# Joining the high and low halves of Strassen products into one 512-column matmul, on PSUM banks that ScalarE fills first

## The chip, the cores and the metric

One Trainium2 chip, one core of it. The metric is the device time of one execution in microseconds (us); lower is better.

## What is computed

A trunk of two layers over one sequence of 512 frames of width 1024. Each layer, cut to what matters:

```
h = x + 1/2 * SwiGLU_1(RMSNorm(x))            # 1024 -> 2 x 2816 -> 1024
u = RMSNorm(h);  u @ w_in -> conv B, C, V | q_down | kv_down | k_rope | gate_conv | gate_mla
h = h + W_o( sigmoid(gate_conv) * conv_branch + sigmoid(gate_mla) * attention_branch )
h = h + 1/2 * SwiGLU_2(RMSNorm(h))
h = h + sigmoid(RMSNorm(h) @ W_pg) * (p[i] @ W_pp)
```

and a last RMSNorm behind both. Everything is float32.

## The kernel before

Activations lie transposed: features on the 128 partitions, the 512 frames along the free dimension, eight tiles `h[0..7]` of 128x512 for the residual. To get float32 accuracy from the faster matmul type, each operand is split into a high part, which is its rounding to that type, and a low part, the remainder. ScalarE makes the high part (the cast at line 70 for weights, line 209 for activations) and VectorE the low one (line 71, line 210). A product of two such operands takes three matmuls: high·high, high·low and low·high (`mm3`, lines 217 to 219).

Weights stream from DRAM in pieces of 128x1024 (`Stream`, buffers `st`, ten of them), are split into `wh` and `wl` (four buffers each), and are used once.

The up and gate projections of the four FFNs, and the gate projections of the mixer, are done by Strassen's method (the variant with seven products and 15 additions) in *quads*: four weight quarters of 128x1024 (`Quad`), each product being 512 rows of weights by 256 output features by 256 frames. Quarters are combined on VectorE (lines 146, 151, 154, 157). The activation side is combined once a stage (`Halved`, which fills `ys[1]` to `ys[7]`). `Sevens.product` issues the 24 matmuls of one product at line 455, each with 256 columns: 4 row tiles, 2 column tiles `w`, 3 parts. `Sevens.step(n, j)` does product `j` of quad `n`. Three PSUM banks serve a quad: `b` gathers products 1, 6, 7 and 4 one after the other, `c` gathers 5 and 3, and `a` has product 2. In between ScalarE copies the running sum out (line 474, after 1, 5 and 6), and VectorE adds it to another bank (line 479) to make an output quarter. Then `finish` (FFN) or `gate` (mixer) scales by the norm's reciprocal root, `r`, applies Silu or Sigmoid, and for the FFN splits the result into `acts`.

Down projections (`down`, 512 columns, bank `pd`) are laid between the products: four feature tiles at a time for one output tile `m`, 12 matmuls. In the mixer `conv_out` (also 12 matmuls) has that place. The order of products is written out by hand: in the FFN loop, for quad `n + 1` and what is left of `n`, it is (n+1,1), (n,7), (n+1,5), (n,4), (n+1,2), (n+1,6), (n+1,3), with 12-matmul pieces after the second, third, fourth and sixth. A scheduler at build time fixes the final order on each engine from what it reckons to be ready, so that matmuls of neighbouring pieces can be interleaved.

The second FFN of each layer (stage names `b0`, `b1`) begins with Strassen products of quads 0 and 1 at once; the first FFN (`a0`, `a1`) and the mixer (`m0`, `m1`) begin with ordinary projections. `e0`, `e1` are the last step of a layer.

All eight PSUM banks are one pool of single tiles (`mp`, `PS`). SBUF has a pool `G` of 60 tiles of 128x512.

Stages on TensorE: a0 from 6.2 us, m0 from 352.6, b0 from 737.8, e0 from 1080.7, a1 from 1135.6, m1 from 1480.0, b1 from 1865.3, e1 from 2208.2.

## Time and profile before

| | |
|---|---|
| median of 3 runs | 2277.62 us (2277.31 to 2277.88) |
| profiled execution, first to last instruction | 2275.7 us (the profile has no other time of it) |
| TensorE matmuls | 14206, busy 2266.7 us |
| VectorE | 2544 instructions, busy 1816.1 us |
| ScalarE | 1751 instructions, busy 1163.2 us |
| Strassen matmuls (line 455) | 8232 of 256 columns |
| DMA | 223.28 MB, mean 98 GB/s |

How to read the rows below. A row of the timeline has start, duration, engine, line, operation, output<-inputs, shape; a bracket at the end has how long the engine sat idle before and what ended it. Matmuls are pipelined: a duration reaches past the start of the next one, so the time that a matmul takes of TensorE is the distance from its start to the next start. A row of a stretch (`A:B`) has its length and then, for each engine (PE, PEld, DVE, ACT, POOL, or those of one line only), the busy time and the number of instructions, and at the end the granted clock, the DMA share and GB/s. A group row has the line, what it does, xcount, and after the bar the busy time, the mean duration in ns and the idle time before. PE is TensorE, PEld its weight loads, DVE VectorE, ACT ScalarE, SP the queue that issues most DMAs.

### The profile page before, as it was taken

What the parts mean: (1) busy time and instruction counts of PE and PEld (TensorE: products, weight loads), DVE (VectorE), ACT (ScalarE), POOL (GpSimd) and SP (SyncE); (2) the same over time, 40 slices, a digit from 0 to 9 for tenths busy, and PEclk for the clock granted to TensorE, in tenths of its full rate; (3) what the DMA queues carried; (4) which work ended last, traced back from release to release, by engine and by line L of the source; (5) the groups of instructions that cost most, each with busy time, mean ns of one, the idle gap of its engine ahead of it and who ended that gap; (6) DMA issues with size and microseconds to landing.
All of it is one profiled execution on the core that took longest, in us unless ns stands there. A gap on an engine that the chain in (4) does not pass through costs nothing.

```text
span 2275.7 us, 34817 instructions
## 1 busy us (share of the span) xinstructions
PE 2266.7 (100%) x14206; PEld 2058.0 (90%) x14206; DVE 1816.1 (80%) x2544; ACT 1163.2 (51%) x1751; POOL 38.1 (2%) x42
## 2 busy tenths in 40 slices
PE   9999999999999999999999999999999999999998
PEld 8999988899888999998899999888998889999987
DVE  8877778877877988877798887767878689878766
ACT  7444445456745644444664444454567465444444
POOL 0000000000200000000000000000001000000000
PEclk9999999999999999999999999999999999999999
DMA  5333343134121333333223333422331214333321
GB/s 195 112 112 95 105 130 102 55 113 130 47 66 56 103 112 111 94 120 122 91 80 97 112 93 118 119 87 74 103 121 47 75 38 138 103 103 93 121 93 38
DMA packets 63375, 223.28 MB, mean 98 GB/s; under 512 B 7280, under 2 KB 7280, under 8 KB 63216
## 3 DMA queue, kind: packets, MB, share of 16 engines
q1 hardware_dynamic: 62640, 220.28, 30.7%
q8 instruction: 111, 1.82, 0.3%
q10 hardware_dynamic: 576, 0.79, 0.1%
q14 instruction: 48, 0.39, 0.1%
HBM read 218.94 MB, written 2.10 MB: 97 GB/s over the span
## 4 chain that ended last, share of the span: by engine, by line
PE 98%; DVE 1%; ACT 0%; issue 0%; DVEq 0%; ACTq 0%
PE a0pd L217 2%; PE a1pd L217 2%; PE b0pd L217 2%; PE b1pd L217 2%; PE b1pd L218 2%; PE b0pd L218 2%; PE a1pd L218 2%; PE a0pd L218 2%; PE b0pd L219 2%; PE a1pd L219 2%; PE a0pd L219 2%; PE b1pd L219 2%; PE m0mop L217 1%; PE m1mop L218 1%; PE m0mop L218 1%; PE e0gp L219 1%
## 5 line engine op out<-in xcount | busy, mean ns | idle before, releaser
L70 ACT CAST wh<-st 128x1024 fp32r<-128x1024 f32 (+1 forms) x458 | 476.8, 1044 | 567.2 <-issue 62.7
L71 DVE TENSOR_TENSOR wl<-st,wh 128x1024 fp32r<-128x1024 f32 (+1 forms) x459 | 555.1, 1211 | 155.0 <-ACT wh L70 154.2
L70 ACT CAST wh<-s 128x1024 fp32r<-128x1024 f32 x98 | 103.0, 1051 | 132.6 <-DVE s L151 8.9
L71 DVE TENSOR_TENSOR wl<-s,wh 128x1024 fp32r<-128x1024 f32 x98 | 119.3, 1218 | 13.5 <-ACT wh L70 13.5
L154 DVE TENSOR_TENSOR st<-st,s 128x1024 f32<-128x1024 f32 x49 | 59.9, 1222 | 1.2
L151 DVE TENSOR_TENSOR s<-s,st 128x1024 f32<-128x1024 f32 x49 | 59.7, 1218 | 0.2
L157 DVE TENSOR_TENSOR st<-st,st 128x1024 f32<-128x1024 f32 x49 | 59.6, 1217 | 0.1
L146 DVE TENSOR_TENSOR s<-st,st 128x1024 f32<-128x1024 f32 x49 | 59.6, 1216 | 0.1
L563 DVE SCALAR_TENSOR_TENSOR h<-b1pd,h 128x512 f32<-128x512 f32 x40 | 27.5, 688 | 10.4 <-PE b1pd L219 10.4
L563 DVE SCALAR_TENSOR_TENSOR h<-b0pd,h 128x512 f32<-128x512 f32 x40 | 27.5, 687 | 9.1 <-PE b0pd L219 9.1
L563 DVE SCALAR_TENSOR_TENSOR h<-a1pd,h 128x512 f32<-128x512 f32 x40 | 27.5, 687 | 7.6 <-PE a1pd L219 7.5
L563 DVE SCALAR_TENSOR_TENSOR h<-a0pd,h 128x512 f32<-128x512 f32 x40 | 27.4, 685 | 6.4 <-PE a0pd L219 6.4
L107 POOL MEMSET wh<- 128x256 f32 x4 | 1.1, 312 | 1189.7 <-DVE wl L71 1189.7
L988 ACT ACTIVATE e1g<-e1pg,e1r 128x512 f32<-128x512 f32 (+1 forms) x9 | 5.4, 641 | 11.9 <-PE e1pg L950 11.9
L992 DVE TENSOR_TENSOR e1g<-e1g,e1in 128x512 f32<-128x512 f32 (+1 forms) x9 | 5.7, 628 | 7.3 <-ACT e1g L988 7.3
L117 DVE TENSOR_TENSOR kl<-st,kh 128x512 fp32r<-128x512 f32 x8 | 5.3, 688 | 7.4 <-ACT kh L116 7.4
L882 DVE TENSOR_TENSOR m1g<-m1mop,m1g 128x512 f32<-128x512 f32 x8 | 5.5, 689 | 5.9 <-PE m1mop L219 5.9
L882 DVE TENSOR_TENSOR m0g<-m0mop,m0g 128x512 f32<-128x512 f32 x8 | 5.5, 689 | 5.5 <-PE m0mop L219 5.5
L300 ACT ACT_TABLE_LOAD x7 | 9.0, 1283 | 0.1
L287 DVE TENSOR_TENSOR e1acc<-e1acc,e1sq 128x512 f32<-128x512 f32 x7 | 4.8, 691 | 4.8 <-ACT e1sq L286 4.3
L709 DVE TENSOR_TENSOR m1g<-m1cop,m1g 128x512 f32<-128x512 f32 x8 | 5.5, 687 | 2.0 <-PE m1cop L219 2.0
L709 DVE TENSOR_TENSOR m0g<-m0cop,m0g 128x512 f32<-128x512 f32 x8 | 5.5, 687 | 2.0 <-PE m0cop L219 2.0
(11249 smaller groups left out, 8792.5 us busy)
## 6 DMA issues: line engine op xcount, KB each, us to landing
st<-in_weights SPq DMA_DIRECT2D x406, 512.0 KB, 3.5
h<-in_x SPq DMA_DIRECT2D x8, 256.0 KB, 5.3
st<-in_weights SPq DMA_DIRECT2D x7, 256.0 KB, 5.3
out<-e1d SPq DMA_DIRECT2D x4, 256.0 KB, 2.1
out<-fh SPq DMA_DIRECT2D x3, 256.0 KB, 2.2
e0pi<-in_p SPq DMA_DIRECT2D x2, 256.0 KB, 3.7
e1pi<-in_p SPq DMA_DIRECT2D x2, 256.0 KB, 3.7
fg<-in_final_row SPq DMA_DIRECT2D x2, 256.0 KB, 4.4
```

The source lines that it names most:

```text
L70: self.nc.scalar.copy(hi[:, w], src[:, w])
L71: last = self.nc.vector.tensor_tensor(lo[:, w], src[:, w], hi[:, w].bitcast(F32), ALU.subtract)
L146: tt(self.s, self.a21, self.a22, ALU.add)
L151: tt(self.s, self.s, self.a11, ALU.subtract)
L154: tt(self.a12, self.a12, self.s, ALU.subtract)
L157: tt(self.a11, self.a11, self.a21, ALU.subtract)
L217: nc.tensor.matmul(ps, wh, vh, start=first, stop=False)
L218: nc.tensor.matmul(ps, wh, vl, start=False, stop=False)
L219: nc.tensor.matmul(ps, wl, vh, start=False, stop=last)
L563: nc.vector.scalar_tensor_tensor(h[m], ps, 0.5, h[m], ALU.mult, ALU.add)
L709: nc.vector.tensor_tensor(gates[m], ps, gates[m], ALU.mult)
L882: nc.vector.tensor_tensor(t, mla_ps[m], t, ALU.mult)
```

## The change

In five of the seven products (1, 2, 3, 4, 6) the high weights meet high and low activations in one matmul of 512 columns, whose output fills a bank: 256 columns of sums with the high part, 256 with the low part. The low weights meet the high part in a second matmul of 256 columns, added onto the first half. Each bank of a product becomes a pair of banks (two column tiles), and an output quarter is the sum of the two halves (`out`: ScalarE copies one half, VectorE adds the other). Products 5 and 7 keep three matmuls of 256 columns (`product`).

Instead of adding a saved sum on VectorE, ScalarE copies the pair `b` onto the seeded pair (`seed`) after product 1 and again after product 6, and products 2, and 5 and 3, accumulate onto that copy. The combination of weight quarters for product 6 is formed in another way, so that 5 needs no `s`. The order in a quad becomes (n+1,1), (n,4), (n+1,2), (n+1,6), (n+1,5), (n+1,7), (n+1,3), with 12-matmul pieces after 1, 2, 6 and 3. The first two quads of the second FFNs (`early`) keep products 5 and 3 on a bank of their own and do product 3 as before.

PSUM is divided outside attention into two pairs for `b`, one seeded pair, and two single banks; inside attention it is eight single banks. High and low parts of the layer inputs, of the query latents, of the rotary key and of the head outputs lie side by side in eight paired buffers (`X`), and `G` has 44 tiles. The transposed probabilities of attention move from `G` to three raw weight buffers. The two halves of each `u` row are split separately. The end of an FFN, the head of the other stages and the order around the mixer's first quad are rearranged for the smaller number of single banks.

```diff
-N_BIG = 60
+N_BIG = 44
+N_PAIR = 8
...
 class Quad:
-    def __init__(self, W, quarters):
-        self.W = W
+    def __init__(self, W, quarters, early):
+        self.W, self.early = W, early
         for q in ("a11", "a21", "a22", "a12"):
             setattr(self, q, W.raw(quarters[q]))
         tt = W.nc.vector.tensor_tensor
         if j == 1:
             return W.split(self.a11)
         if j == 2:
             return W.split(self.a12)
-        if j == 6:
-            tt(self.s, self.s, self.a11, ALU.subtract)
-            return W.split(self.s)
+        if j == 4:
+            return W.split(self.a22)
         if j == 3:
             tt(self.a12, self.a12, self.s, ALU.subtract)
             return W.split(self.a12)
-        if j == 7:
+        if self.early:
+            if j == 5:
+                self.s = W.buffer("s")
+                tt(self.s, self.a21, self.a22, ALU.add)
+                return W.split(self.s)
+            if j == 6:
+                tt(self.s, self.s, self.a11, ALU.subtract)
+                return W.split(self.s)
             tt(self.a11, self.a11, self.a21, ALU.subtract)
             return W.split(self.a11)
-        return W.split(self.a22)
+        if j == 6:
+            tt(self.a11, self.a11, self.a21, ALU.subtract)
+            self.s = W.buffer("s")
+            tt(self.s, self.a22, self.a11, ALU.subtract)
+            return W.split(self.s)
+        if j == 5:
+            tt(self.a21, self.a21, self.a22, ALU.add)
+            return W.split(self.a21)
+        return W.split(self.a11)
...
+        def eight(self):
+            self.close()
+            self.single = self.pool("mp", 8)
+        def paired(self):
+            self.close()
+            self.chain, self.seeded, self.single = self.pool("bp", 2), self.pool("ap", 1), self.pool("mp", 2)
...
+    def two(pool, name):
+        return pool.tile([P, 1024], F32, tag="bb", name=name).rearrange("p (w t) -> p w t", t=512)
+    def PB(name):
+        return two(banks.chain, name)
+    def PA(name):
+        return two(banks.seeded, name)
+    def halves(t):
+        return [t[:, 0, :], t[:, 1, :]]
+    def X(name):
+        t = xp.tile([P, 1024], F32R, tag="x", name=name).rearrange("p (a t) -> p a t", t=S)
+        v = HiLo((t[:, 0, :], t[:, 1, :]))
+        v.pair = t
+        return v
...
+    def split(src, name, scale=None, paired=False):
+        v = X(name) if paired else (G(name + "h", F32R), G(name + "l", F32R))
+        split_to(*v, src, scale)
+        return v
...
+            self.ys[7].append((th[:, right], tl[:, right]))
+            for p_, at in ((2, left), (3, right)):
+                self.ys[p_].append(self.both(xs[k], at))
+            for p_, at in ((6, left), (4, right)):
+                v = G(f"{self.name}u{j}_{p_}", F32R).rearrange("p (a t) -> p a t", t=H)
+                last = split_to(v[:, 0, :], v[:, 1, :], u[:, at])
+                self.ys[p_].append((v[:, 0, :], v))
...
+        def joint(self, ps, d, j):
             hi, lo = d.pop(("part", j), None) or d["w"].part(j)
-            for k, (vh, vl) in enumerate(self.ys[j]):
+            for k, (vh, pair) in enumerate(self.ys[j]):
+                for w in range(2):
+                    at = slice((2 * k + w) * P, (2 * k + w + 1) * P)
+                    nc.tensor.matmul(ps[:, w, :].rearrange("p (a t) -> p a t", t=self.H), hi[:, at], pair, start=j == 1 and k == 0,
+                                     stop=False, skip_group_check=True)
+                    nc.tensor.matmul(ps[:, w, :self.H], lo[:, at], vh, start=False, stop=k == 3, skip_group_check=True)
+        def product(self, ps, d, j, start=False):
+            hi, lo = d.pop(("part", j), None) or d["w"].part(j)
+            for k, v in enumerate(self.ys[j]):
+                vh, vl = v if j in (5, 7) else (v[0], v[1][:, 1, :])
                 for w in range(2):
                     at = slice((2 * k + w) * P, (2 * k + w + 1) * P)
                     for i, (a_, b_) in enumerate(((hi, vh), (hi, vl), (lo, vh))):
-                        nc.tensor.matmul(ps[:, w, :], a_[:, at], b_, start=j in (1, 5, 2) and w + k + i == 0,
-                                         stop=w + k + i == 6, skip_group_check=True)
+                        nc.tensor.matmul(ps[:, w, :], a_[:, at], b_, start=start and w + k + i == 0,
+                                         stop=k == 3 and i == 2, skip_group_check=True)
+        def seed(self, n, what):
+            d = self.todo[n]
+            d[what] = PA(f"{self.name}{n}{what}")
+            nc.scalar.copy(d[what].rearrange("p w t -> p (w t)"), d["b"].rearrange("p w t -> p (w t)"))
+        def out(self, n, ps, f, c):
+            t = self.tile(n, f"o{f}{c}")
+            nc.scalar.copy(t, ps[:, :, self.H:])
+            nc.vector.tensor_tensor(t, ps[:, :, :self.H], t, ALU.add)
+            self.done(n, f, c, t, t)
         def step(self, n, j):
+            d, H, early = self.quad(n), self.H, n < self.early
+            tt = nc.vector.tensor_tensor
+            if j == 1:
+                d["b"] = PB(f"{self.name}{n}b")
+                self.joint(d["b"], d, j)
+                if not (early and n):
+                    self.seed(n, "a")
+            elif j == 2:
+                self.joint(d["a"], d, j)
+                self.out(n, d.pop("a"), 0, 0)
+                if n + 1 < self.early:
+                    self.seed(n + 1, "a")
+            elif j == 6:
+                self.joint(d["b"], d, j)
+                if early:
+                    d["u"] = [self.tile(n, f"u{w}") for w in range(2)]
+                    for w in range(2):
+                        nc.scalar.copy(d["u"][w], d["b"][:, :, w * H:(w + 1) * H])
+                    tt(d["c5"], d["c5"], d["u"][1], ALU.add)
+                else:
+                    self.seed(n, "d")
+            elif j == 5:
+                d["c5"] = self.tile(n, "c5")
+                if early:
+                    d["c"] = PS(f"{self.name}{n}c").rearrange("p (w t) -> p w t", t=H)
+                    self.product(d["c"], d, j, True)
+                    nc.scalar.copy(d["c5"], d["c"])
+                else:
+                    self.product(d["d"][:, :, H:], d, j)
+                    nc.scalar.copy(d["c5"], d["d"][:, :, H:])
+            elif j == 7:
+                self.product(d["b"][:, :, :H], d, j)
+                t = d.pop("c5")
+                tt(t, d["b"][:, :, :H], t, ALU.add)
+                self.done(n, 1, 1, t, t)
+            elif j == 3 and early:
+                self.product(d["c"], d, j)
+                t, l = d.pop("u")
+                tt(t, t, l, ALU.add)
+                tt(t, d.pop("c"), t, ALU.add)
+                self.done(n, 0, 1, t, t)
+            elif j == 3:
+                self.joint(d["d"], d, j)
+                self.out(n, d.pop("d"), 0, 1)
             else:
+                self.joint(d["b"], d, j)
+                self.out(n, d.pop("b"), 1, 0)
...
+        f_last = (np_ - 3) // 2 * 4
+        downs = []
+        def fill():
+            if downs:
+                m, f0 = downs.pop(0)
+                down(m, f0, f0 + 4)
+        def next_quad(n):
+            for i, j in enumerate((1, None, 4, 2, None, 6, None, 5, 7, 3, None)):
+                if j is None:
+                    if i < 10 or downs and downs[0][1] < f_last:
+                        fill()
+                    continue
+                step(n if j == 4 else n + 1, j)
+                if j == 6 and n % 2:
+                    downs.extend((m, 2 * n - 2) for m in range(KD))
...
+            behind = sums
+            for n, j in ((0, 2), (0, 6), (0, 3), (0, 7), (1, 2), (0, 4), (1, 6), (1, 3), (1, 7)):
+                with tc.issue_after(behind):
+                    step(n, j)
+                behind = W.last_split
+            n0 = 1
...
+        for n in range(n0, np_ - 1):
+            next_quad(n)
+        f0 = f_last
+        left = [m for m in range(KD) if (m, f0) in downs]
+        assert len(left) == len(downs)
+        spare = halves(PA(f"{name}pd"))
+        for m in left[:3]:
+            pds[m] = down(m, f0, f0 + 4, spare[0] if len(pds) == 2 else None, last=False)
+            if len(pds) == 1:
+                step(np_ - 1, 4)
+        if beside:
+            beside()
+        for m in left[3:4] + [m for m in range(KD) if m not in left[3:4]]:
+            if m in left[3:]:
+                down(m, f0, nf, spare[1] if m == left[3] else None)
+            else:
+                down(m, f0 + 4, nf, pds.get(m), first_=m not in pds)
...
+            pss = halves(PB(f"{name}{nm}p")) + [PS(f"{name}{nm}p2")]
+            return [proj(W.col("w_in", l, c0 + k * P, D), xs, None, pss[k]) for k in range(width // P)]
...
+            if last:
+                ys.row(k, xs)
+                step(0, 1)
...
+            if last:
+                step(0, 2)
+                step(0, 6)
...
+        for j in (5, 7, 3):
+            step(0, j)
...
+            for n_, j_, n_out in ((n + 1, 1, n > 0), (n, 4, 0), (n + 1, 2, 0), (n + 1, 6, 1), (n + 1, 5, 0), (n + 1, 7, 0),
+                                  (n + 1, 3, 1)):
                 step(n_, j_)
+                conv_outs(n_out)
+                if (n_, j_) == (n_last, 6):
+                    qc = [split(t, f"{name}qn{k}", paired=True) for k, t in enumerate(qt)]
                     kvc = [split(t, f"{name}kvn{k}") for k, t in enumerate(kvt)]
-                    krh, krl = split(krt, name + "kr")
-                if (n_, j_) == (n_last, 3):
-                    pairs[0].q_rope()
+                    krh, krl = split(krt, name + "kr", paired=True)
+        conv_outs(len(outs))
+        pairs[0].q_rope()
+        step(n_last, 4)
+        banks.eight()
...
+            return split(ps, n + "o", paired=True)
...
+        banks.paired()
         for m in range(KD):
             ps = proj(W.col("w_o", l, m * P, D), merged, f"{name}wop{m}")
...
+            pg, pp = halves((PA if m % 3 == 2 else PB)(f"{name}gp{m}"))
             proj(W.col("w_ple_gate", l, m * P, D), xs, None, pg)
```

More of the change, by code (lines that the diff above doesn't have):

```diff
@@ L321, in trunk_kernel @@
     nc.scalar.activation(warm, eps_t, AF.Copy)
-    idle = PS("idle")
-    for i in range(12):
-        nc.tensor.matmul(idle[:, :P], ones.bitcast(F32), ones.bitcast(F32), start=True, stop=True)
+    idle, one = PA("idle"), ones.bitcast(F32)
+    for i in range(8):
+        nc.tensor.matmul(idle[:, 0, :P], one, one, start=True, stop=True)
+    nc.tensor.matmul(idle[:, 1, :].rearrange("p (a t) -> p a t", t=P), one, one.unsqueeze(1).to_broadcast([P, 4, P]),
+                     start=True, stop=True)
     pt_w = [max(2, NT - j) * P for j in range(NT)]
@@ L384, in __init__, with both @@
             self.half = {}
+        @staticmethod
+        def both(v, at):
+            return v[0][:, at], v.pair[:, :, at]
         def row(self, j, xs):
@@ L400, in own @@
                 split_to(th[:, left], tl[:, left], t[:, left])
-            self.ys[1].append(tuple(v[:, left] for v in xs[j]))
+            self.ys[1].append(self.both(xs[j], left))
             self.ys[5].append((th[:, left], tl[:, left]))
@@ L443, in split @@
-        def split(self, n, j):
-            if n not in self.todo:
-                self.todo[n] = self.quad(n)
-            self.todo[n]["part", j] = self.todo[n]["w"].part(j)
-        def product(self, ps, d, j):
-            hi, lo = d.pop(("part", j), None) or d["w"].part(j)
-            for k, (vh, vl) in enumerate(self.ys[j]):
+            if n not in self.todo:
+                cs = self.columns(n)
+                quarters = {f"a{a_ + 1}{b_ + 1}": [(self.w, self.l, (4 * b_ + k) * P, c) for k in range(4) for c in cs[a_]]
+                            for a_ in range(2) for b_ in range(2)}
+                self.todo[n] = {"w": Quad(W, quarters, n < self.early)}
@@ L646, in lat_norm @@
             return ts
[L648 removed]
+        pkv = halves(PB(name + "kvp"))
+        projs([W.col("w_in", l, o_kv + k * P, D) for k in range(KL // P)], xs, pkv)
         pkr = PS(name + "krp")
@@ L884, in mixer @@
             merged.append(split(t, f"{name}mg{m}"))
+        banks.paired()
         for m in range(KD):
@@ L936, in ple_last @@
         name = f"e{l}"
+        banks.eight()
         pt = ple_parts(l, name)
```

250 lines of the change are left out of this document (106 added, 144 removed).

## The prediction

> **What bounds the kernel now.** I read the page's busy shares, clock row and chain first, then the waits of TensorE, then its timeline.
>
> ```profile
> span 2275.7 us, 34817 instructions
> ...
> PE 2266.7 (100%) x14206; PEld 2058.0 (90%) x14206; DVE 1816.1 (80%) x2544; ACT 1163.2 (51%) x1751; POOL 38.1 (2%) x42
> ...
> PEclk9999999999999999999999999999999999999999
> ...
> PE 98%; DVE 1%; ACT 0%; issue 0%; DVEq 0%; ACTq 0%
> ...
> PE idle L325 <- DVE hpi L255: 1.0, 1, 1.0
> ```
>
> TensorE is busy for the whole span at the full granted clock, 98% of the chain is its own work, and its one recorded wait is 1.0 us before the warm-up. So nothing another engine saves can show, and every nanosecond taken off a matmul does. A busy row is no proof that matmuls stand close together, since each lasts longer than its successor waits; the starts decide that:
>
> ```profile
> 300.48 0.40 PE L217 MATMUL a0pd<-a0a13h,wh 128*128 128x512 f32 x1
> ...
> 302.30 0.39 PE L219 MATMUL a0pd<-a0a15h,wl 128*128 128x512 f32 x1
> 302.53 0.28 PE L455 MATMUL a010a<-a0x4h,wh 128*128 128x256 f32 x1
> 302.64 0.28 PE L455 MATMUL a010a<-a0x4l,wh 128*128 128x256 f32 x1
> ...
> 1002.40 0.28 PE L455 MATMUL b09b<-b0u0h,wh 128*128 128x256 f32 x1
> ...
> 1005.28 0.40 PE L217 MATMUL b0pd<-b0a12h,wh 128*128 128x512 f32 x1
> 1005.51 0.40 PE L218 MATMUL b0pd<-b0a12l,wh 128*128 128x512 f32 x1
> ```
>
> From 1002.40 to 1005.28 lie the 24 matmuls of one Strassen product: 2.88 us, 120 ns each for 256 columns. From 300.48 to 302.30 lie 8 matmuls of 512 columns: 227.5 ns each. Twice the columns cost 107.5 ns more, so 12.5 ns of every matmul do not depend on its length. That is what the change attacks.
>
> **The change part by part.**
>
> *Fewer matmuls.* A product now has, for each of 4 row tiles and 2 column tiles, three 256-column matmuls (high·high, high·low, low·high). In a joint product the first two become one of 512 columns; the columns streamed stay the same.
>
> ```profile
> L154 DVE TENSOR_TENSOR st<-st,s 128x1024 f32<-128x1024 f32 x49 | 59.9, 1222 | 1.2
> ...
> 0.00:2276.00 2276.00, 1014.34 (x8232) 1009.95 (x8232) 1.00 0.31 98
> ```
>
> The first row (the subtraction of product 3, once a quad) counts 49 quads; the second is line 455 over the whole span, and its 8232 matmuls are 49 x 7 x 24. In 45 quads five products become joint. The first two quads of each second FFN keep product 3 as it was, so 4 quads have four. 45 x 5 + 4 x 4 = 241 joint products, 241 x 8 = 1928 matmuls gone. Inside runs of one length each is worth 12.5 ns, 24.1 us together. Joint products alternate lengths, so I look at the changes of length: behind a 512 the 256 takes 302.53 to 302.64, behind a 256 the 512 takes 1005.28 to 1005.51, so a pair is 0.34 us against 0.36, 20 ns saved, on starts rounded to 10 ns. I take 14 ns, nearer the value averaged over many instructions: 1928 x 14 = 27.0 us. Ends: 24.1 and, by the rounded starts, 38.6, which I do not believe.
>
> The Trainium skill, TensorE: Matmul & The Clock Gate, section "Wait — 56ns, not 53.3ns?", puts the fixed part of a warm matmul at about 2.5 ns. By that the 1928 would be worth an estimated 4.8 us. The trace disagrees: its starts leave 12.5 ns.
>
> *Seeds on ScalarE.* Each of the 45 quads gains two copies of two PSUM banks onto two others (after products 1 and 6), and swaps three 512-element copies for four. No row shows ScalarE writing PSUM. The nearest:
>
> ```profile
> 245.92 0.28 PE L455 MATMUL a08b<-a0u3h,wl 128*128 128x256 f32 x1
> 246.04 0.40 PE L217 MATMUL a0pd<-a0a8h,wh 128*128 128x512 f32 x1
> ...
> 248.79 0.28 PE L455 MATMUL a08c<-a0x4h,wh 128*128 128x256 f32 x1
> ...
> 246.17 1.05 ACT L70 CAST wh<-st 128x1024 fp32r<-128x1024 f32 x1 [0.94 <-PE a08b L455]
> ...
> 247.13 0.58 ACT L474 COPY a08c<-a08b 128x512 f32<-128x512 f32 x1
> ```
>
> A 1024-element cast takes 1.05 us and its successor starts 0.96 later; 512 from PSUM take 0.58; so I take 1.0 us for a seed, between 0.58 and twice that. These rows are also the pattern itself: a product on bank b ends at 245.92, a cast for later weights runs first, and the copy starts at 247.13. In the new order product 6 is followed by a down projection or a convolution output, 12 matmuls, here 246.04 to 248.79, and only then by product 5, which adds onto the seed. The seed would be ready at 248.13: 0.66 us to spare. The seed after product 1 has another product as cover as well. Cost 0, hidden by the 12 matmuls; above 1.66 us it would show. A gain is excluded, since the copy only adds a wait. ScalarE's extra is 45 x (2 x 1.0 + 0.58) = 116 us, and 4 for one seed in each of the four early quads, on 1163: 56%. Queued behind a late seed would be the next weight cast, which has three products of lead.
>
> *VectorE.* Each quad needs one more addition of 512 elements (four evacuations instead of three, product 4 included), and the same four subtractions on the weights.
>
> ```profile
> 0.00:2276.00 2276.00, 101.09 (x147) 1.00 0.31 98
> ...
> 800.00:1050.00 250.00, 250.00 (x1723) 233.65 (x1722) 199.74 (x242) 108.90 (x145) 0.00 (x0) 1.00 0.35 109
> ```
>
> The first row is line 479, 147 such additions: 0.69 us each, so 34 us more, 80% to 82%. The second is a steady FFN stretch (PE, PEld, DVE, ACT busy): VectorE at 199.74 of 250, with 8 quads in it some 5.5 more, still under 83%. Cost 0. Splitting each u row in two halves adds fixed parts on both engines for four rows a stage; taken at 0 inside the same slack.
>
> *Fewer single banks.* Eight PSUM banks in one pool become two pairs for bank b, one seeded pair and two singles outside attention. Where three singles are wanted within a few us, TensorE waits. Two places show it:
>
> ```profile
> 743.79 0.39 PE L297 MATMUL b0ps<-b0al,ones 128*128 128x512 f32 x1
> ...
> 746.90 0.28 PE L455 MATMUL b01c<-b0t0h,wh 128*128 128x256 f32 x1
> ...
> 748.27 0.70 ACT L302 ACTIVATE b0ms<-b0ps,eps_t 128x512 f32<-128x512 f32 x1
> ...
> 384.10 0.69 DVE L637 TENSOR_TENSOR m0qt<-m0qp,m0r 128x512 f32<-128x512 f32 x1 [0.67 <-PE m0qp L219]
> ...
> 384.36 0.40 PE L217 MATMUL m0Cp<-m0x0h,wh 128*128 128x512 f32 x1
> ...
> 386.56 0.68 ACT L302 ACTIVATE m0kvms<-m0kvps,eps_t 128x512 f32<-128x512 f32 x1
> ...
> 458.06 0.28 PE L455 MATMUL m0g0c<-m0t3h,wh 128*128 128x256 f32 x1
> 458.19 0.28 PE L455 MATMUL m0g1b<-m0x0h,wh 128*128 128x256 f32 x1
> ...
> 459.21 0.28 PE L455 MATMUL m0g1b<-m0x1h,wh 128*128 128x256 f32 x1
> 459.32 0.29 PE L455 MATMUL m0g0c<-m0t3l,wh 128*128 128x256 f32 x1
> ```
>
> At the head of the second FFN, bank c of quad 0 and the norm's sums hold both singles. The sums are last read at 748.27 + 0.70 = 748.97 behind a table load, while product 5 of quad 1 wants a bank at 746.90 - 0.1 (the joint product before it is shorter). That is 2.2 us, twice: 4.4. Ends 0 (TensorE's order is woven by readiness: from 458.19 to 459.21 seven matmuls of quad 1 stand between two of quad 0's bank c, so other products may fill the gap) and 4.4. In the mixer the first C projection (384.36) needs the third query bank, read until 384.79: 0.45 us, twice, 0.9; if it took the kv norm's bank, read until 386.56 + 0.68, 2.9 each. What then comes late is the weight cast behind it, with buffers to spare.
>
> *Attention.* It keeps eight banks. The head outputs now share eight paired buffers with the three query latents and the rotary key. Heads 0 to 3 find four free; 4 to 6 take those of the queries, done with once pair 3 is projected, ahead of head 4; head 7 takes the key's after the last scores.
>
> ```profile
> 548.00:658.00 110.00, 110.00 (x653) 98.43 (x651) 90.93 (x219) 77.50 (x174) 18.13 (x16) 1.00 0.20 63
> ...
> 564.95 0.28 PE L803 MATMUL m0s00p<-m0h0kn0h,m0h0qn0h 128*128 128x256 f32 x1
> ...
> 568.17 0.40 PE L217 MATMUL m0h1qr<-m0qn0h,wh 128*128 128x512 f32 x1
> ```
>
> The stage's VectorE is at 90.93 of 110, ScalarE at 77.50, TensorE without a gap. I take 0, hidden by that order; the upper end is one set of score matmuls (564.95 to 568.17, 3.2 us) waiting once for heads 4 and 7 of each layer, 12.9, should their late buffers hold up banks.
>
> *Order and DMA.* Products move to 1, 4 of the last quad, 2, 6, 5, 7, 3; the same transfers are issued on SP's queue, quarters are released earlier than before (a21 after product 5), and three of the ten raw buffers serve attention, where DMA is 0.20 busy. Cost 0, hidden by that slack. The warm-up has the same TensorE time.
>
> *The sum.* Against the profiled span: 2275.7 - 27.0 + 4.4 + 0.9 = 2254.0. The median of the runs, 2277.62, lies 1.9 above the span, so 2255.9; I say 2256.
>
> **The rivals.**
>
> *Partly eaten by banks.* The mechanism holds, but the attention end (12.9) and the kv bank (4.9 more) are paid, in all 17.8 or in good part: 2262 to 2273. For it: two singles instead of eight. Against: the same weaving.
>
> *Little of the fixed part goes.* If most of the 12.5 ns belongs to something that the 512 still pays (its two halves come from two runs), say all but a fifth, 24.1 / 5 = 4.8 us are saved, and 2277.6 - 4.8 + 5.3 = 2278, no change. Against: contiguous 512s pay it once, at 227.5 ns. The Trainium skill's 2.5 ns (TensorE: Matmul & The Clock Gate, the section above) would end here too.
>
> *Two pieces stream no faster than two matmuls.* The moving operand of a joint product 1, 2 or 3 is two runs of 256 columns, 512 apart; no row shows such a one. If the 512 then costs 240 ns, nothing is saved: 2277.6 + 5.3 = 2283. Against: the operand is contiguous within each run.
>
> *Slower: the seed after product 6 comes late.* Place: product 5 of 45 quads. It costs 45 us for each us that the seed exceeds 1.66; the 21.7 us left of the gain are gone at 1.66 + 0.48 = 2.14 us. If a copy into PSUM takes 2.4 us, or as much ScalarE work stands ahead of it, 45 x 0.74 = 33 us: 2289. For it: no price is known, and every quad repeats it. Against: 0.58 us for half as much.
>
> **How the numbers follow.** Main case 64% (2250 to 2262, its own range), partly eaten 14%, better than 2250 3%: faster 81%. Smaller fixed part 4%, stalls that cancel the gain 2%: within 0.2% (4.6 us, about what a measurement of this kernel can tell) 6%. Two pieces 4%, late seed 9%: slower 13%. The range 2249 to 2271 takes in the main case and nearly all of the eaten one.
>
> **What would show it.** Right: TensorE's count near 12,270 and joint pairs at 0.346 us; TensorE without waits before product 5; a gap near product 5 of quad 1 at the head of each second FFN. Wrong: gaps before products 2, 5 or 3 that repeat every quad, seed copies above 1.7 us, 512-column matmuls of joint products 240 ns apart, or gaps in the attention stage.

## The result, and the profile after

The changed kernel takes 2320.35 us (median of 4 runs, 2317.42 to 2320.87) against 2277.6: a ratio of 1.0185, 95% interval 1.0172 to 1.0197. It is 43 us slower; 2256 was forecast, and 2271 was the upper end. Its profiled execution spans 2318.8 us, 43.1 more than that of before.

Busy shares, clock and chain of the profile's page after:

```profile
span 2318.8 us, 31379 instructions
...
PE 2273.8 (98%) x12272; PEld 1960.4 (85%) x12272; DVE 1853.1 (80%) x2628; ACT 1270.3 (55%) x1922; POOL 40.4 (2%) x42
...
PE 90%; DVE 6%; ACT 2%; issue 1%; DMA 0%; SPq 0%; ACTq 0%; DVEq 0%
```

1934 matmuls are gone, and yet TensorE's busy time is 7 us higher: the matmuls that are left take longer, part of them at half clock, as shown below. The chain tells where else to look: VectorE now holds 6% of it, for 1%. The waits of TensorE after (waiting tile and line, what ended it: us in total, times, longest us):

```profile
PE a02b L530 <- DVE a0u L272: 7.4, 4, 2.7
PE m0kvp L281 <- DVE wl L72: 5.9, 1, 5.9
PE m0h0kn L279 <- DVE m0g3o L553: 3.5, 1, 3.5
PE b11c L542 <- ACT b1ms L363: 1.8, 1, 1.8
PE b01c L542 <- ACT b0ms L363: 1.8, 1, 1.8
PE e0gp L279 <- DVE e0g L1077: 1.4, 1, 1.4
```

Before there was one row of 1.0 us. None of these is at product 5 or 2 of a steady quad, where the forecast looked for the danger: they stand where stages begin. The third kind of loss is the clock (stretch, length, busy time and instructions of PE, PEld, DVE, ACT, POOL, granted clock, DMA share, GB/s):

```profile
52.00:62.00 10.00, 7.04 (x18) 5.16 (x19) 8.54 (x20) 6.29 (x12) 0.00 (x0) 0.50 0.01 2
369.00:377.00 8.00, 6.25 (x16) 4.95 (x17) 5.70 (x6) 1.33 (x3) 0.56 (x2) 0.57 0.60 199
```

Behind waits the granted clock drops to half: at 51.9 us for 10.2 us, at 369.4 for 6.8, at 577.6, 775.5 and 1912.2 for 3.4 each; before, none did between the warm-up and the last 6 us. The Trainium skill, TensorE: Matmul & The Clock Gate, section "What's actually happening", gives half rate after an idle window of about 3.4 us, with windows that run freely. The trace agrees with the windows: the starts and ends of these five stretches lie on one grid of 3.413 us. It adds that less idle time can do: at 775.5 and at 1912.2 a single wait of 1.8 us, with no other in the 9 us ahead, was enough; behind the same waits of e2, below, the clock stayed full.

To share out the 43.1 us I took the distance from every matmul's start to the next and compared it with the 227.5 ns (512 columns) and 120 ns (256) of undisturbed runs. The counts alone save 24.1 us. Against that stand 42.0 us more in gaps of over 40 ns, 13.8 us of half clock, and 12.3 us of small excess; the first matmul of a0 comes 1.0 earlier. (How much of a wait inside a half-clock stretch is called a gap is a choice: another count gives 45.9 and 9.9 in place of 42.0 and 13.8, with the same sum.) By stage the gaps grew by 7.0 us in a0, 12.7 in m0, 9.5 in b0, 9.3 in b1, and by nothing in a1, where the forecast's picture held: that stage went from 344.4 to 342.1 us.

### The profile page after: what moved, and what is told of

Same layout as the page of the kernel before. It is cut to its first block, busy times and chain, and to the rows that moved or that the text cites. A ratio compares the mean times of both kernels' runs of the same rounds, so it can differ in the third digit from the quotient of the medians.

```text
span 2318.8 us, 31379 instructions
## 1 busy us (share of the span) xinstructions
PE 2273.8 (98%) x12272; PEld 1960.4 (85%) x12272; DVE 1853.1 (80%) x2628; ACT 1270.3 (55%) x1922; POOL 40.4 (2%) x42
## 4 chain that ended last, share of the span: by engine, by line
PE 90%; DVE 6%; ACT 2%; issue 1%; DMA 0%; SPq 0%; ACTq 0%; DVEq 0%
PE a1pd L279 2%; PE b1pd L279 2%; PE b0pd L279 2%; PE a1pd L281 2%; PE b1pd L281 2%; PE b0pd L281 2%; PE a1pd L280 2%; PE b1pd L280 2%; PE b0pd L280 2%; DVE wl L72 2%; PE a0pd L279 1%; PE a0pd L280 1%; PE a0pd L281 1%; PE e0gp L279 1%; PE e0gp L280 1%; PE e0gp L281 1%
## 5 line engine op out<-in xcount | busy, mean ns | idle before, releaser
L71 ACT CAST wh<-st 128x1024 fp32r<-128x1024 f32 (+1 forms) x503 | 524.7, 1046 | 658.6 <-PE a1pd L280 23.1
L72 DVE TENSOR_TENSOR wl<-st,wh 128x1024 fp32r<-128x1024 f32 (+1 forms) x504 | 611.2, 1214 | 253.8 <-ACT wh L71 252.9
L71 ACT CAST wh<-s 128x1024 fp32r<-128x1024 f32 x53 | 55.7, 1051 | 71.7 <-DVE s L158 4.0
L72 DVE TENSOR_TENSOR wl<-s,wh 128x1024 fp32r<-128x1024 f32 x53 | 64.7, 1221 | 11.6 <-ACT wh L71 11.4
L150 DVE TENSOR_TENSOR st<-st,s 128x1024 f32<-128x1024 f32 x49 | 59.7, 1219 | 0.0
L163 DVE TENSOR_TENSOR st<-st,st 128x1024 f32<-128x1024 f32 x45 | 55.1, 1225 | 1.3
L165 DVE TENSOR_TENSOR s<-st,st 128x1024 f32<-128x1024 f32 x45 | 54.9, 1219 | 0.1
L168 DVE TENSOR_TENSOR st<-st,st 128x1024 f32<-128x1024 f32 x45 | 54.9, 1221 | 0.0
L530 PE MATMUL a02b<-a0u,wh 128*128 128x512 f32 x16 | 8.0, 521 | 7.4 <-DVE a0u L272 7.4
L1117 PE MATMUL e1pg<-kh,e1x 128*128 128x512 f32 (+1 forms) x40 | 13.9, 349 | 0.0
L279 PE MATMUL m0Cp<-m0x,wh 128*128 128x512 f32 x32 | 12.7, 396 | 1.2 <-DVE m0qt L788 0.8
L1118 PE MATMUL e1pg<-kl,e1x 128*128 128x512 f32 (+1 forms) x40 | 13.9, 347 | 0.0
L1119 PE MATMUL e1pg<-kh,e1x 128*128 128x512 f32 (+1 forms) x40 | 13.9, 347 | 0.0
L279 PE MATMUL m1Cp<-m1x,wh 128*128 128x512 f32 x32 | 12.7, 395 | 0.7 <-DVE m1b L867 0.4
```

The source lines that it names most:

```text
L71: self.nc.scalar.copy(hi[:, w], src[:, w])
L72: last = self.nc.vector.tensor_tensor(lo[:, w], src[:, w], hi[:, w].bitcast(F32), ALU.subtract)
L150: tt(self.a12, self.a12, self.s, ALU.subtract)
L163: tt(self.a11, self.a11, self.a21, ALU.subtract)
L165: tt(self.s, self.a22, self.a11, ALU.subtract)
L168: tt(self.a21, self.a21, self.a22, ALU.add)
```

## The experiments

Theory: the joint products do save, but less than 14 ns for each matmul gone, because 512s and 256s alternate; the rest is lost where a stage begins, since work of VectorE, ScalarE and banks that used to be covered no longer is. Main rival: the loss lies in every quad (seeds, VectorE's 34 us). All ratios below are against before at 2277.4 to 2277.6 us on the same chip as the run; lengths of stages are from the profiled executions.

**The lengths** (e4). In a joint product all eight 512s go first, then the eight 256s.

```diff
 for k, (vh, pair) in enumerate(self.ys[j]):
     for w in range(2):
         nc.tensor.matmul(..., hi[:, at], pair, ...)
+for k, (vh, pair) in enumerate(self.ys[j]):
+    for w in range(2):
         nc.tensor.matmul(..., lo[:, at], vh, ...)
```

> In a joint product all eight 512-column matmuls come first and then the eight of 256 columns, instead of in turn; the same matmuls. Theory A (a change of length costs): the 512s take 227 ns and the 256s 120, a pair 347 instead of 353 on average, 1928 x 6 ns = 11 us, 2320.4 to about 2309; the low parts are also wanted 1.8 us later, which can take off some of the waits at the heads of the second FFNs. Theory B (the 512 with two halves is dearer by itself): the 512s stay at 235 to 240 ns, the time stays above 2317.

Measured: 2306.51 us, 13.8 less (ratio to before 1.0124, interval 1.0107 to 1.0141). The timeline of the changed kernel, and below it the same part of the regrouped one (start, duration, engine, line, output<-inputs, shape, count):

```profile
1329.72 0.40 PE L530 MATMUL a16b<-a1x,wh 128*128 128x512 f32 x1
1329.95 0.28 PE L532 MATMUL a16b<-a1x,wl 128*128 128x256 f32 x1
...
1332.19 0.40 PE L279 MATMUL a1pd<-a1a4h,wh 128*128 128x512 f32 x1
```

```profile
1322.85 1.98 PE L530 MATMUL a16b<-a1x,wh 128*128 128x512 f32 x8
1324.67 1.11 PE L535 MATMUL a16b<-a1x,wl 128*128 128x256 f32 x8
1325.62 0.40 PE L279 MATMUL a1pd<-a1a4h,wh 128*128 128x512 f32 x1
```

Seven alternating pairs take 2.47 us, 353 ns each, against 360 for the three matmuls of before: 7 ns saved, not 14. Regrouped, eight 512s take 1.82 us, 227.5 ns each, and eight 256s 0.95, 119 ns: 346 a pair. The 512s over two separate runs (`a1x`) cost as much as those over one (`a1u`) when lengths alternate (353.5 against 353.1 ns a pair, averaged over the trace), and 1.6 ns more when regrouped (229.1 against 227.5). So it is the alternation that costs 5 to 7 ns a pair, and hardly the operand. A single change of length costs nothing: averaged over the trace of before, a 512 between a 256 and another 512 takes 233.6 ns, and a 256 between a 512 and another 256 takes 113.8, together 347.4, as in runs of one length; in alternation the two take 236.1 and 117.2. The small excess of the whole kernel fell from 12.5 to 1.1 us; what is left of the 13.8 came off gaps.

**Rotary work at the first mixer** (e2). The 24 VectorE instructions that make the rotary tables, which run in one block at the end of a0, are handed out over the last quads.

```diff
 def rotary():
     nc.vector.tensor_scalar(...)
+    yield
...
 def fill():
+    if beside and n_done[0] >= 4 and side[-1:] != ["last"]:
+        side.append(next(beside))
```

> The 25 VectorE operations of the rotary tables are spread over the last quads of a0 instead of standing together at its end; the two Sin operations stay where they were. Theory (a few uncovered places): the wait of 5.9 us in the mixer's first projection and the half-clock stretch behind it come from weight low parts queued behind the rotary and norm work on VectorE; m0 falls from 401.0 us to about 390, the time from 2320.4 to about 2310. Rival (steady load): VectorE has no room in the quads, a0 grows by as much as m0 falls, the time stays within 3 us of 2320.

Measured: 2310.62 us, 9.7 less (1.0142, 1.0127 to 1.0157). The 5.9 us wait of `m0kvp` is gone, and so is the half clock at 369. Its cause in the changed kernel stands in VectorE's timeline, where no low weight part (`wl`) is made for 26 us:

```profile
342.93 1.22 DVE L72 TENSOR_TENSOR wl<-st,wh 128x1024 fp32r<-128x1024 f32 x1
344.07 0.42 DVE L421 TENSOR_SCALAR turns<-ang 128x512 f32<-128x512 f32 x1
...
369.46 1.23 DVE L72 TENSOR_TENSOR wl<-st,wh 128x1024 fp32r<-128x1024 f32 x1
```

**The order at the head of the second FFNs** (e3). Product 5 of quad 1 goes behind product 2 of quad 0, so that the norm's sums have left their bank.

```diff
     step(1, 1)
-    step(1, 5)
...
-for n, j in ((0, 2), (0, 6), ...
+for n, j in ((0, 2), (1, 5), (0, 6), ...
```

> At the head of each second FFN product 5 of quad 1 comes after product 2 of quad 0 instead of before it, so that it no longer wants a single bank while the norm's sums hold one. Theory A (the bank): the wait of 2.0 us and the half-clock stretch behind it go, 3.5 us in b0 and in b1, 2320.4 to about 2313. Theory B (VectorE is the bound at this place, 32.2 of 33.0 us busy): the wait turns up at the weight low parts, b0 and b1 fall by less than 1 us each, the time stays above 2318.

Measured: 2315.29 us, 5.1 less (1.0165, 1.0149 to 1.018); b0 and b1 take 348.5 and 347.5 us in place of 351. The two waits on `ms` are gone, but waits on low weight parts grow (1.4 us at `b02b`, for 0.6): behind the bank stood VectorE.

**Two additions of each early quad on GpSimd** (e6), on top of the last edit, to lighten VectorE there.

```diff
-tt(d["c5"], d["c5"], d["u"][1], ALU.add)
+nc.gpsimd.tensor_tensor(d["c5"], d["c5"], d["u"][1], ALU.add)
...
-tt(t, t, l, ALU.add)
+nc.gpsimd.tensor_tensor(t, t, l, ALU.add)
```

> On top of the run with the other order at the heads of the second FFNs (2315.3 us): the two additions that each early quad has on SBUF alone (c5 with u, and the two halves of u) go from VectorE to GpSimd. Theory (VectorE is the bound at the heads, and its added operations cost there one for one): 4 x 0.69 us a stage come off, b0 and b1 fall by up to 2.7 us each, 2315.3 to about 2310 to 2312. Rival (latency of single operations counts, GpSimd's longer ones cost more than they free): no fall, 2315 or above.

Measured: 2322.6 us (1.0196, 1.0179 to 1.0213), 7.3 more than without it. One of the eight additions on GpSimd, and the low weight parts on VectorE between 764 and 854 us (busy, mean ns, idle before):

```profile
L575 POOL TENSOR_TENSOR b01c<-b01c,b01u 128x512 f32<-128x512 f32 x1 | 2.2, 2168 | 20.3 <-ACT b01u L574 20.3
```

```profile
L72 DVE TENSOR_TENSOR wl<-st,wh 128x1024 fp32r<-128x1024 f32 x21 | 26.7, 1276 | 3.9 <-ACT wh L71 3.7
```

An addition of 0.69 us on VectorE takes 1.3 to 2.2 on GpSimd. The low parts took 1276 ns on average against 1219 without, and that is the doing of one: at 786.63, beside two of these additions, it took 2.37 us, and the others their 1.22. TensorE then waited 2.6 us for the chain that runs through it (`b01b` for `b01c`). So this run shows that those additions lie on a chain, and does not settle whether VectorE's sum of work is the bound.

**The first half-step.** Before, the four whole gate/up products ran first and covered the rows `t` and `u`; the change reads two of them out ahead of the rows. First edit (e1): the fourth product whole again, ahead of the quads, on one more pair of banks.

```diff
     activate(1)
+    pss[3] = whole(3)
+    projs(cs[3], xs, pss[3])
 for j in range(early, KD // 2):
     ys.row(j, xs)
...
```

> In the first FFN (a0) the fourth gate and up projections are done whole before the first quad again, on a pair of chain banks, as the kernel before had them. Theory (a few uncovered places): in the changed kernel these projections wanted single banks that were still held, so product 6 of quad 2 came up 11 us before its u rows; with the cover back the waits of 7.4 us on the u rows and the half-clock stretch behind them go, a0 falls from 357.5 us to about 344, the time from 2320.4 to about 2306. Rival (steady load): VectorE and ScalarE are too busy everywhere with the added copies and additions, so the wait only moves to a later product of a0, which stays above 354, the time above 2317.

Measured: 2314.58 us, 5.8 less (1.0161, 1.0146 to 1.0177). But a0 got no shorter, 359.2 us for 357.8. The gain is that of m0, 395.4 for 401.2, where the wait of `m0h0kn` is gone: luck, whose cause is found further below. In a0 the wait on `u` shrinks from 7.4 to 3.1 us, and a new one stands at a seed:

```profile
PE a02d L542 <- ACT a02d L548: 6.2, 1, 6.2
```

Second edit (e5): the rows ahead of the read-outs as well.

```diff
+for j in range(early, KD // 2):
+    ys.row(j, xs)
 if first:
-    activate(0)
...
+    activate(0)
     activate(1)
-for j in range(early, KD // 2):
-    ys.row(j, xs)
...
```

> In a0 the four rows of combined activations are written ahead of the first two activations (as in the kernel before), and the fourth gate and up projections are done whole ahead of the quads. The run with the cover alone moved the wait from the u rows to a seed (6.2 us), since the rows still stood on VectorE behind the activations, from 42 to 62 us, where the kernel before did them from 23 to 44 us. Theory (order on VectorE): with the rows first neither wait is left, a0 falls from 357.5 to about 344 us, the time from 2320.4 to about 2306. Rival (one seeded pair is too few at this place): the seed after product 6 still waits for the pair to be read out, over 3 us, and a0 stays above 350.

Measured: 2316.88 us, 3.5 less (1.0173, 1.0158 to 1.0188), where 2306 was expected; this expectation fell. a0 takes 358.8 us where 344 was expected, and the gain is again m0's, 394.7. The wait had moved again, to the bank pair of the fourth product, which VectorE now reads out late:

```profile
PE a0p L279 <- ACT a0gn L655: 7.6, 1, 7.6
```

**These together.** Rows first, rotary spread, product 5 later, lengths grouped (e7); and the same with the additions on GpSimd (e8).

> Four repairs together: rows and fourth projection first in a0, rotary operations spread over the quads, the other order at the heads of the second FFNs, 512-column matmuls ahead of the 256-column ones. If the places are separate the gains add up: 2320.4 - 14 - 10 - 5 - 14 = 2277, the kernel before. If they compete for VectorE the sum is not reached: above 2285.

> The four repairs and the additions on GpSimd. Theory (VectorE-bound heads): 2 to 5 us below the run with the four, 2272 to 2275, faster than the kernel before. Rival: no better than it.

Measured: 2288.18 us (1.0047, 1.0032 to 1.0062), 32.2 less than the changed kernel. The single gains of the four edits, 3.5 + 9.7 + 5.1 + 13.8, sum to 32.1: they add up. Still 2277 had been expected, with 14 us from the edit of a0. That edit gave a0 nothing here either: a0 takes 355.4 us, and 355.2 in e4, without it. With GpSimd 2292.36 (1.0065, 1.005 to 1.008), where 2272 to 2275 was expected. Of small excess e7 has 1.0 us left; 12 us of gaps are left in a0 and 8.1 in each second FFN.

**VectorE at the head of the second FFNs.** Two runs beside e7. In one (e12), two additions of each early quad are left out, so that its sums lack two of their parts; in the other (e10) the second FFNs begin with two whole gate/up products, as the third FFN does.

```diff
-tt(d["c5"], d["c5"], d["u"][1], ALU.add)
...
-tt(t, t, l, ALU.add)
```

> Beside e7 (2288.18 us) one thing: of each of the two first quads of the half-steps behind the mixers two additions on VectorE of 0.69 us are left out (the values computed there lack two of their parts; all other work stays). In each half-step VectorE is spared 4 x 0.69 = 2.8 us in the stretch where it is busy without a break. Theory (VectorE's work is the bound of that stretch): each half-step gets 2.0 to 2.8 us shorter, 2282.6 to 2284 us. Rival (what is waited for is the chain from ScalarE's high part to VectorE's low part of one weight, not the sum of the work): under 1 us in all, 2287 to 2288.5 us.

```diff
-ffn(l, "ffn2", f"b{l}", early=3)
+ffn(l, "ffn2", f"b{l}")
```

> Beside e7 (2288.18 us) one thing: the two half-steps behind the mixers begin, as the third half-step does, with two whole gate and up products of 96 matmuls in place of their first quad of Strassen products. These need 16 tiles split for 192 matmuls and no combination of weights. By count that is 2.0 us more of matmuls in each (the third half-step without its excess is 338.8 us, these are 336.8). Theory (the head is bound by VectorE, which had 20 us out of 20 between 785 and 805 us in e7): the 8.1 us of waits in each fall to about 1 us, each half-step ends up at 339 to 340 us against 345.4, in all 10 to 12 us less: 2277 us. Rival (the waits come from the time at which the rows and the norm are ready behind the mixer): they stay, and the added matmuls come on top: 2290 to 2292 us.

Measured: 2283.94 us for the first, 4.2 less, and 2275.95 (0.9994, 0.9985 to 1.0002) for the second, 12.2 less. Of 5.5 us of VectorE's time left out, 4.2 came off the end: its sum of work was most of the bound. A chain through those two additions, as with GpSimd, could give the same, but TensorE's largest wait at that head of e7 is for low weight parts:

```profile
PE b01c L560 <- DVE wl L72: 1.6, 2, 0.8
```

The head in the combined kernel, and below it with whole products (columns as in the stretches above):

```profile
785.00:805.00 20.00, 18.35 (x108) 15.74 (x107) 20.00 (x27) 13.25 (x20) 0.00 (x0) 1.00 0.36 105
```

```profile
785.00:805.00 20.00, 20.00 (x118) 17.60 (x117) 19.76 (x27) 12.18 (x18) 0.00 (x0) 1.00 0.40 132
```

In the first VectorE works 20 us out of 20 and TensorE 18.35; with whole products TensorE does not wait there at all, at the price of 2.0 us more of matmuls by their lengths in each of these stages. Both stages fall from 345.6 to 339.7 us.

**The bank of the fourth product.** In a0 it goes onto the seeds' pair, which is free then, and so ahead of the read-outs (e9); e11 adds the whole products to that, and e14 also reads that pair out second in place of third.

```diff
-activate(0)
-activate(1)
-pss[3] = whole(3)
+pss[3] = halves(PA(f"{name}p3"))
...
+for f in (0, 1, 3):      # e14: (0, 3, 1)
+    activate(f)
```

> Beside e7 (2288.18 us) one thing: the fourth whole gate and up product of the first half-step goes onto the pair of banks that otherwise takes the seeds, which nothing holds at that time, in place of a pair that has to be read out by VectorE first. Theory (the 7.6 us wait of that product, and the 1.8 us of half clock behind it, come from the banks alone): TensorE goes on, the half-step gets 8 to 9 us shorter, 2280 us. Rival (VectorE is the bound of that head: three activations and four rows of weight splits have to be done by 60 us whatever TensorE does first): the wait comes back at the first seed or at a weight split, the gain is under 3 us, 2285 to 2288 us.

> Both of the foregoing edits on e7 (2288.18 us). Theory (both waits are of this order of work and not of the idea of the change): the two gains add, 2267 to 2270 us, and the change is then faster than the kernel before (2277.6 us). Rival: they do not add, or one of them is not there: 2276 us or more.

> Beside e11 (2277.28 us) one thing: of the whole products of the first half-step the fourth, which has the banks of the seeds, is read out second in place of third. Theory (the 5.1 us that product 2 of the first quad waits for its seed are the order of the read-outs alone): VectorE has read those banks at 52 in place of 57 us, the seed is there at 53 to 54, 4 us of the wait go, 2273 us. Rival (VectorE's sum of work up to 60 us sets the end of that stretch): a later product waits in its place, 2276 to 2277.5 us.

Measured: 2290.01 (1.0054, 1.0042 to 1.0067), 2277.28 (0.9999, 0.999 to 1.0008) and 2274.18 (0.9987, 0.9978 to 0.9996). The first is a miss of another kind than either theory: a0 itself got 5.0 us shorter, 5.1 us of wait having moved to the first seed, but m0 got 5.7 longer. The second is close to the sum of its two edits, 1.8 more and 12.2 less than e7, and so missed the 2267 to 2270 expected of it. The order of the read-outs then took 3.1 us off, where 4 was expected. The m0 part was the wait of the first key projection:

```profile
PE m0h0kn L279 <- DVE m0g3o L571: 4.1, 1, 4.1
```

**Why that wait comes and goes.** It is in the changed kernel, absent in e1, e5 and e7, and back in e9, e11 and e14. The three without it hand out one pair of banks more in a0. The pairs alternate, so by the kernel's order of handing them out an odd number more moves the last gate pair of m0 from banks 0 and 1, where the eight single banks begin, to 2 and 3 (the traces do not show bank numbers). One edit to move it, on the changed kernel (e13) and on e14 (e15):

```diff
 banks.eight()
+if l == 0:
+    for i in range(2):
+        PS(f"{name}skip{i}")
```

> The changed kernel (2320.35 us) with one thing: in the first mixer the first two of the eight single banks are passed over once when the pairs are given up, so that the first key projection takes the other pair's banks. Theory (the wait of 3.5 us, and the half clock of 3.4 us behind it, come from the bank that the count of pairs handed out happens to leave last written): both go, 3.5 + 1.7 = 5.2 us, 2315 us. Rival (VectorE is late there, and what comes next has to wait for it as well): the wait moves on to the next projection, 2318 to 2320.5 us.

> e14 with the two single banks passed over as in e13. Theory: both gains add, 4.1 us of wait and 1.6 of half clock less than e14, 2268 us, which is faster than the kernel before (2277.6 us) by 0.4%. Rivals: if only the bank's part holds 2271.5 us, if only the order's part holds 2273 us, if neither 2277 us.

Measured: 2319.42 (1.0185, 1.0171 to 1.0198) and 2273.94 (0.9985, 0.9976 to 0.9994), where 2315 and 2268 were expected: no change. The wait of `m0h0kn` on the last gate pair stands as it was (3.5 and 4.1 us), so the edit did not move the banks, probably because tiles that nothing writes take none; it tells nothing about the theory. The next one moves a warm-up matmul (e16, the changed kernel) or all of them (e17, e14) onto a pair of the other kind:

```diff
-nc.tensor.matmul(idle[:, 0, :P], one, one, start=True, stop=True)
+nc.tensor.matmul(idle[:, 0, :P] if i else PB("flip")[:, 0, :P], one, one, start=True, stop=True)
```

> The changed kernel (2320.35 us) with one of the warm-up matmuls put onto a pair of its own, so that up to the first attention every pair has the other two banks, and the last gate pair banks 2 and 3 in place of 0 and 1, with which the attention begins. Theory (bank): the wait of 3.5 us and the half clock behind it go, 3.5 + 1.7 = 5.2 us, 2315 us. Rival (VectorE late): the wait moves to the next projections, 2318 to 2320.5 us.

> e14 (2274.18 us) with the warm-up matmuls on a pair of the other kind, to the same end. Theory (bank): 4.1 us of wait and 1.6 to 2.9 us of half clock go, 2268 us, 0.4% faster than the kernel before. Rival (VectorE late): 2272 to 2274 us.

Measured: 2313.92 us (1.0158, 1.0144 to 1.0172), 6.4 less than the changed kernel, of which m0 has 5.4; and 2267.66 us (0.9956, 0.9942 to 0.9969), 6.5 less than e14. The wait is gone in both, and none took its place: it came from the pair that the count had assigned, and VectorE was not late for anything else. In the changed kernel the place reads:

```profile
572.85 0.28 PE L532 MATMUL m0g3b<-m0u,wl 128*128 128x256 f32 x1
576.60 0.50 PE L279 MATMUL m0h0kn<-m0kvn0h,wh 128*128 128x512 f32 x1 [3.47 <-DVE m0g3o L553]
```

The last variant is faster than the kernel before by 0.44%. Its page and the head of its waits:

```profile
span 2265.1 us, 31147 instructions
...
PE 2248.2 (99%) x12176; PEld 1952.5 (86%) x12176; DVE 1818.2 (80%) x2586; ACT 1260.2 (56%) x1892; POOL 40.4 (2%) x42
```

```profile
PE a02d L560 <- ACT a02d L566: 1.7, 1, 1.7
PE e0gp L279 <- DVE e0g L1104: 1.4, 1, 1.4
PE a02a L545 <- ACT a02a L566: 1.3, 1, 1.3
```

## Why the prediction was wrong, step by step

The sum was 2254.0 us for the span, and the span is 2318.8: 64.8 us off. 15.2 of them are the matmuls (27.0 expected, 24.1 less 12.3 found), 36.7 are gaps (42.0 for 5.3), 13.8 are half clock, and the start gives 1.0 back; 0.1 is rounding.

- *Fewer matmuls.* The mechanism was right and the count (12,272 for "near 12,270"). The term was mis-sized: 14 ns a matmul was read from two starts rounded to 10 ns, on the longer side of 12.5, where the alternating pair gives 7. Each of those two rows is a single change of length, and neither has another length both ahead of it and behind it, as in a joint product. Ordered by length nearly all of the 12.5 of the long runs came back. The 2.5 ns of the Trainium skill (TensorE: Matmul & The Clock Gate, section "Wait — 56ns, not 53.3ns?") was not borne out: in the regrouped kernel, runs of one length start every 120.2 and 227.9 ns on average, 12.5 of them independent of length.
- *Seeds on ScalarE.* Right in the steady quads, in price (1.0 us taken, measured in 94 copies) and in cover. The one row for all of them, in the changed kernel:

```profile
0.00:2320.00 2320.00, 94.36 (x94) 0.99 0.29 96
```

  The slower rival, a late seed in every quad, did not come. At the head of a0, where ScalarE stands behind VectorE's read-outs, seeds were late in several variants.
- *VectorE at cost 0.* This is the step that failed most. The total was right (1853.1 for 1850). But its slack was read from 800 to 1050 us, where down projections, which need few weights for their matmuls, lie between the products. At the head of b0 there are none yet, and VectorE was full there already before, with TensorE just kept fed. The sum also counts one more addition a quad, and an early quad has three more, 6 for 3 (204 in the kernel for 147: 45 + 4 x 3 more), which is 4.1 us in each second FFN at just this place. After, the same part starves TensorE:

```profile
770.00:802.00 32.00, 32.00 (x258) 31.51 (x257) 31.59 (x41) 18.47 (x27) 0.00 (x0) 1.00 0.46 135
```

```profile
797.00:830.00 33.00, 29.74 (x178) 25.05 (x178) 32.23 (x41) 19.34 (x27) 0.00 (x0) 1.00 0.34 112
```

  The first row is of before, the second of after. The whole products, which replace 8.1 us of waits by 2.0 us of matmuls in each stage, and the left-out additions show it. The bank of product 5 has a part in it: from 764 to 797 VectorE stood idle for 6.0 us behind ScalarE's high parts, and ScalarE for 3.8 us at the copy of product 5, which had waited for the bank. e3, which takes the bank's wait away, gains 2.7 and 3.5 us in the two stages, of the 9.5 and 9.3 by which their gaps had grown.
- *Fewer single banks.* Right where it was priced: 1.8 us for 2.2 at product 5 of quad 1, 0.8 and 0.3 for 0.45 at the first C projections. It missed the places where pairs, not singles, are short: the fourth product of a0, and the first key projection of m0, which was in no term.
- *The rearranged heads.* The front part names them and the sum does not price them. a0's cover for the rows and m0's for the rotary work went with them, 7.4 and 5.9 us of wait; with the banks and half clock these two stages lost 30.5 us of the 55.8 in gaps and clock.
- *Half clock.* Not foreseen: with TensorE never idle before, the clock had looked like a constant. It makes a wait cost more than itself: 1.8 us brought 3.4 us of half clock.
- *Attention, order and DMA.* 0 was right inside attention; m1 has 1.5 us more of gaps.

What stays open: 5.0 us of gaps in a0 and a wait of 1.4 at e0 in the last variant were not followed up, nor how much the kernel before would gain from a better order of its own.

## What to carry to other kernels

Where an engine is full, slack has to be read at the stage's head and not from its steady part: VectorE at 80% overall was at 99% there, and 4.2 of the 5.5 us taken off it again came off the end. When a bank budget is cut, list every place where a buffer is handed over and price each, whichever pool it comes from. Order matmuls by length. Test edits one at a time, and read each gain by stage and not from the total alone: several losses of up to 13.8 us hid a gain that was there, and two edits of a0 seemed to gain 5.8 and 3.5 us that came from another stage.

## What was unexpected of the hardware

Matmuls of 512 and 256 columns in alternation cost 5 to 7 ns a pair beyond the two lengths (353 against 346 ns in the rows shown), while a single change of length cost nothing (347.4 ns for the two beside it); whether an operand is one run or two made at most 1.6 ns. Waits of which the longest took 1.8 to 7.6 us were followed by 3.4 to 13.7 us of half clock, on a grid of 3.413 us. GpSimd took 1.3 to 2.2 us for an addition that VectorE does in 0.69, and one VectorE instruction beside it took 2.37 us in place of 1.22.
